# Row normalisation on one core: both loads ahead of the entry barrier and both stores on SyncE, in place of a first store on ScalarE

## The chip, the cores and the metric

The kernel runs on one core of one Trainium2 chip. The metric is device time in microseconds (us). A profiled execution has a span, from its first recorded instruction to its last; the measured time is a little longer than the span.

The core has compute engines that run their own instruction streams (here ScalarE, called ACT, and VectorE, called DVE, do the work), a SyncE (SP) that only issues transfers and waits, and 16 DMA engines that move data between the main memory (HBM) and the on-chip memory (SBUF). An engine that issues a transfer puts it into a queue of its own: q1 is SyncE's, q10 is ScalarE's.

## The reference

```python
def setup_inputs():
    batch, dim = 1024, 4096
    return {"x": np.random.randn(batch, dim).astype(np.float32), "axis": -1, "eps": np.float32(1e-12)}

def reference(x, axis, eps):
    norm = np.sqrt(np.sum(x ** 2, axis=axis, keepdims=True) + eps)
    return (x / norm).astype(np.float32)
```

Every one of the 1024 rows is divided by its Euclidean length. 16.78 MB are read and as much is written.

## The kernel before

The 1024 rows are 128 partitions times 8 rows. They are handled in two groups of R = 4 rows per partition; each group is one tile of 128 x 16384 floats (64 KB per partition), one load and one store.

```python
groups = []
for i in range(n_tiles):                       # n_tiles = 2
    g = RowGroups(nc, io, stats, scratch, D, R, eps_t)
    load = nc.sync.dma_start(out=g.flat(), in_=x_t[i])
    if i == 0:
        first_load_to_front(nc, load.ins)
    groups.append(g)

for i, g in enumerate(groups):
    g.square_dve(R - 1)      # sum of squares of row 3, on VectorE
    g.square_act(0)          # ... of row 0, on ScalarE
    g.norm(0)                # square root on ScalarE, reciprocal on VectorE
    g.scale(0)               # row times reciprocal, on VectorE, in place
    g.square_act(1)
    g.norm(1)
    g.norm(R - 1)
    g.scale(1)
    g.scale(R - 1)
    g.square_act(2)
    g.norm(2)
    if i < n_tiles - 1:
        g.scale_by_both(2)   # 7/8 of the row on ScalarE, 1/8 on VectorE
    else:
        g.scale(2)
    queue = nc.scalar if i < n_tiles - 1 else nc.sync
    store = queue.dma_start(out=out_t[i], in_=g.flat())
gpsimd_waits_for_last_store(nc, store.ins)
```

(The comments are added here.) A program starts with an entry barrier, at which every engine reports and waits for the others. The first load is moved ahead of SyncE's report to it:

```python
def first_load_to_front(nc, load):
    def move(program):
        blocks = program.main_func.blocks
        entry = blocks[0].instructions
        # ... cut: return if it is there already; find the load in its block (body, at)
        before = next(
            n for n, i in enumerate(entry)
            if i.engine == mybir.EngineType.SP and isinstance(i, mybir.InstDrain)
        )
        entry.insert(before, body.pop(at))
    nc.at_finalize(move)
```

At the end of the program SyncE waits for everything but the last store, and GpSimd alone waits for the last store (`gpsimd_waits_for_last_store`); this part is not changed.

Load 0, load 1, store 0 and store 1 are the names used below for the four transfers.

Of the kernel before, what the change touches and what calls it, by code (L numbers as in the profile page):

```python
# [79 lines left out]
        )  # L80


def first_load_to_front(nc, load):

# [6 lines that stand above are left out]
        if any(i.name == load.name for i in entry):  # L93
            return
        body = next(
            b.instructions
            for b in blocks
            if any(i.name == load.name for i in b.instructions)
        )
        at = next(n for n, i in enumerate(body) if i.name == load.name)  # L100
        assert not body[at].sync_info.on_wait
        before = next(
            n
            for n, i in enumerate(entry)
# [5 lines that stand above are left out]
# [72 lines left out]
@with_exitstack  # L182
def kernel(
    ctx: ExitStack,
    tc: tile.TileContext,
    x: bass.AP,
    axis: bass.AP,
    eps: bass.AP,
    out: bass.AP,
):  # L190
    nc = tc.nc
    P = nc.NUM_PARTITIONS

    assert isinstance(axis, int) and axis in (-1, len(x.shape) - 1)
    eps = float(eps)

    x = x.flatten_outer_dims()
    out_flat = out.flatten_outer_dims()
    N, D = x.shape
    R = 4  # L200
    assert N % (P * R) == 0
    n_tiles = N // (P * R)
    x_t = x.rearrange("(p t r) d -> t p (r d)", t=n_tiles, r=R)
    out_t = out_flat.rearrange("(p t r) d -> t p (r d)", t=n_tiles, r=R)

    io = ctx.enter_context(tc.tile_pool(name="io", bufs=n_tiles))
    scratch_pool = ctx.enter_context(tc.tile_pool(name="scratch", bufs=1))
    stats = ctx.enter_context(tc.tile_pool(name="stats", bufs=n_tiles))

    eps_t = scratch_pool.tile([P, 1], F32)  # L210
    nc.vector.memset(eps_t, eps)  # L211
    sq_act = scratch_pool.tile([P, D], F32)
    sq_dve = scratch_pool.tile([P, D], F32)
    scratch = {"act": sq_act, "dve": sq_dve}

    groups = []
    for i in range(n_tiles):
        g = RowGroups(nc, io, stats, scratch, D, R, eps_t)
        load = nc.sync.dma_start(out=g.flat(), in_=x_t[i])
        if i == 0:  # L220
            first_load_to_front(nc, load.ins)
        groups.append(g)

    for i, g in enumerate(groups):
        g.square_dve(R - 1)
        g.square_act(0)
        g.norm(0)
        g.scale(0)
# [8 lines that stand above are left out]
            g.scale_by_both(2)  # L237
        else:
            g.scale(2)
        queue = nc.scalar if i < n_tiles - 1 else nc.sync  # L240
        store = queue.dma_start(out=out_t[i], in_=g.flat())
    gpsimd_waits_for_last_store(nc, store.ins)


# [33 lines left out]
```

## Time and profile before

| | |
|---|---|
| time, median of 3 runs | 82.57 us (82.54 to 82.77) |
| span of the profiled execution | 80.7 us |
| bytes read from HBM / written to it | 16.78 MB / 16.78 MB |
| share of the DMA engines' span, q1 / q10 | 72.8% / 25.0% |
| load 0 issued | 0.00 us |
| load 1 issued | 0.78 us |
| compute on group 0 begins | 21.81 us |
| store 0 issued, on ScalarE | 38.71 us |
| compute on group 1 begins | 41.12 us |
| store 1 issued, on SyncE | 56.53 us |

Times within an execution count from the start of the span. In the profile's lines, "L33" is a line of the kernel, "ACTq" and "SPq" are issues of transfers by ScalarE and SyncE, a bracket at the end of a timeline line gives the idle time before the instruction and what ended it. A line of waits gives who waited for whom, then the total in us, how often, and the longest. In the strips of 40 slices each digit is the busy share of a fortieth of the span, in tenths.

### The profile page before, as it was taken

The page shows a single profiled execution, that of the slowest core. Times are in us where ns is not written, and L with a number is a line of the kernel's source. Part 1 is how long each engine was busy: PE and PEld are TensorE (multiplying, and loading weights), DVE is VectorE, ACT ScalarE, POOL GpSimd, SP SyncE. Part 2 cuts the span into 40 slices and gives each one's busy share as a digit, 9 for nine tenths or more (in the row PEclk, how much of TensorE's full clock was granted, in tenths as well). Part 3 has the DMA queues.
Part 4 walks back from the last instruction along what each step waited for, and adds up shares of the span by engine and source line. Part 5 has one row for each costly group of instructions (what it writes and reads, how often), then busy time and mean ns, then how long its engine had stood idle before and what let it go on. Part 6 is the DMA issues. An engine that isn't in the chain of part 4 may idle for free.

```text
span 80.7 us, 93 instructions
## 1 busy us (share of the span) xinstructions
DVE 26.8 (33%) x21; ACT 29.8 (37%) x23; POOL 0.2 (0%) x4
## 2 busy tenths in 40 slices
DVE  0000000000199599940069899979000000000000
ACT  6000000000199999989169699970000000000000
POOL 0000000000000000000000000000000000000000
DMA  9099999299999299999199909999938999938990
GB/s 520 32 487 520 520 520 455 97 487 520 520 520 455 97 487 520 520 520 487 65 487 520 520 32 487 520 520 520 520 162 357 520 520 520 520 162 357 520 520 0
DMA packets 576, 33.55 MB, mean 416 GB/s; under 512 B 64, under 2 KB 64, under 8 KB 64
## 3 DMA queue, kind: packets, MB, share of 16 engines
q1 hardware_dynamic: 432, 25.17, 72.8%
q10 hardware_dynamic: 144, 8.39, 25.0%
HBM read 16.78 MB, written 16.78 MB: 416 GB/s over the span
## 4 chain that ended last, share of the span: by engine, by line
DMA 50%; ACT 10%; DVE 9%; issue 0%
DMA xt<-in_x_dram 50%; ACT sq_act L33 9%; DVE sq_dve L42 6%; DVE xt L64 3%; ACT rstd L53 1%; DVE rstd L59 0%
## 5 line engine op out<-in xcount | busy, mean ns | idle before, releaser
L33 ACT ACTIVATE sq_act<-xt 128x4096 f32<-128x4096 f32 x6 | 21.6, 3608 | 22.2 <-DMA xt<-in_x_dram 22.2
L42 DVE SCALAR_TENSOR_TENSOR sq_dve<-xt 128x4096 f32<-128x4096 f32 x2 | 8.8, 4424 | 26.1 <-DMA xt<-in_x_dram 26.1
L64 DVE TENSOR_SCALAR xt<-xt,rstd 128x4096 f32<-128x4096 f32 x7 | 16.5, 2354 | 0.2
L72 ACT ACTIVATE xt<-xt,rstd 128x3584 f32<-128x3584 f32 x1 | 3.3, 3282 | 0.2 <-DVE rstd L59 0.2
L53 ACT ACTIVATE rstd<-ssq,eps_t 128x1 f32<-128x1 f32 x8 | 2.1, 290 | 0.9 <-DVE sq_dve L42 0.8
L59 DVE RECIPROCAL rstd<-rstd 128x1 f32<-128x1 f32 x8 | 1.3, 160 | 2.4 <-ACT rstd L53 2.4
L33 ACT ACT_TABLE_LOAD x1 | 1.3, 1283 | 0.8 <-PEq L259 0.8
L53 ACT ACT_TABLE_LOAD x1 | 1.3, 1283 | 0.0
L33 ACT ACTIVATION_READ_ACCUMULATOR sq_act<-xt 128x1 f32 x6 | 1.1, 185 | 0.0
L78 DVE TENSOR_SCALAR xt<-xt,rstd 128x512 f32<-128x512 f32 x1 | 0.5, 486 | 0.0
L211 DVE MEMSET eps_t<- 128x1 f32 x1 | 0.1, 59 | 0.9 <-PEq L259 0.9
L42 DVE DVE_READ_ACCUMULATOR sq_dve<-xt 128x1 f32 x2 | 0.2, 82 | 0.0
L259 POOL MEMSET const-bfloat16-1.0<- 128x1 bf16 x1 | 0.1, 101 | 0.0
L259 POOL MEMSET const-uint8-127<- 128x1 uint8 x1 | 0.1, 101 | 0.0
L259 POOL MEMSET const-float32-0.0<- 128x1 f32 x1 | 0.1, 98 | 0.2 <-issue 0.2
L259 POOL MEMSET const-float32-1.0<- 128x1 f32 x1 | 0.1, 98 | 0.0
## 6 DMA issues: line engine op xcount, KB each, us to landing
xt<-in_x_dram SPq DMA_DIRECT2D x2, 31.0
out_dram<-xt ACTq DMA_DIRECT2D x1, 24.9
out_dram<-xt SPq DMA_DIRECT2D x1, 24.0
```

Of the source, the lines that this page charges most:

```text
L33: self.nc.scalar.activation(out=sq_a, in_=self.x[:, r], func=ACT_F.Square, accum_out=self.ssq[:, r : r + 1],)
L42: self.nc.vector.scalar_tensor_tensor(out=sq_v, in0=self.x[:, r], scalar=1.0, in1=self.x[:, r], op0=ALU.mult, op1=ALU.mult, accum_out=self ...
L53: self.nc.scalar.activation(out=self.rstd[:, r : r + n], in_=self.ssq[:, r : r + n], func=ACT_F.Sqrt, bias=self.eps_t,)
L59: self.nc.vector.reciprocal(out=self.rstd[:, r : r + n], in_=self.rstd[:, r : r + n])
L64: self.nc.vector.tensor_scalar_mul(out=self.x[:, r], in0=self.x[:, r], scalar1=self.rstd[:, r : r + 1])
L72: self.nc.scalar.activation(out=self.x[:, r, :cut], in_=self.x[:, r, :cut], func=ACT_F.Copy, scale=rstd,)
L78: self.nc.vector.tensor_scalar_mul(out=self.x[:, r, cut:], in0=self.x[:, r, cut:], scalar1=rstd)
L211: nc.vector.memset(eps_t, eps)
L259: nc = _bacc.Bacc("TRN2", target_bir_lowering=False, num_devices=1)
```

## The change

Both loads are now moved ahead of SyncE's report to the entry barrier, and both stores are issued by SyncE. Before, only the first load was ahead of the barrier, and the first store was issued by ScalarE, right behind the scale that it shares with VectorE. The purpose is to have the second load queued as early as the first, and to keep ScalarE's stream free of transfers.

```diff
-def first_load_to_front(nc, load):
+def to_front(nc, load):
 ...
         load = nc.sync.dma_start(out=g.flat(), in_=x_t[i])
-        if i == 0:
-            first_load_to_front(nc, load.ins)
+        to_front(nc, load.ins)
         groups.append(g)
 ...
-        queue = nc.scalar if i < n_tiles - 1 else nc.sync
-        store = queue.dma_start(out=out_t[i], in_=g.flat())
+        store = nc.sync.dma_start(out=out_t[i], in_=g.flat())
     gpsimd_waits_for_last_store(nc, store.ins)
```

In the compiled program SyncE issues load 0 and load 1, then takes part in the barrier, then issues store 0 (which waits for VectorE and ScalarE) and store 1. ScalarE's stream loses its one transfer, and the scheduler also places the instructions of its second group differently: before, the first square is followed by two square roots, the first of which waits for VectorE's square; after, it is followed by one square root, which waits for ScalarE alone, and the other of the two comes after the second square.

## The prediction

> **What bounds the kernel now.** I read the page first, its busy times and its 40 slices, because they tell at once whether an engine or the transfers carry the span.
>
> ```profile
> span 80.7 us, 93 instructions
> DVE 26.8 (33%) x21; ACT 29.8 (37%) x23; POOL 0.2 (0%) x4
> DVE  0000000000199599940069899979000000000000
> ACT  6000000000199999989169699970000000000000
> DMA packets 576, 33.55 MB, mean 416 GB/s; under 512 B 64, under 2 KB 64, under 8 KB 64
> HBM read 16.78 MB, written 16.78 MB: 416 GB/s over the span
> ```
>
> No compute engine is busy for half of the span. Both are idle from the start to slice 10 and from slice 28 to the end. 33.55 MB must move, and 416 GB/s over 80.7 us is all of it. So I ask whether the transfers ever pause. The page's DMA row has digits between 0 and 9 that look like pauses, but rows of 64 KB are booked whole at their start, so a slice of 2 us holds one round of them or none; I don't read that row. I took the packet records of the same trace instead (each has a queue, a start, a duration and a size) and sorted the 512 packets of 64 KB into 32 rounds of 16, one per engine. Summarised, with times from the span's start:
>
> ```
> round  what                        starts         mean took
> 1      load 0, first row           1.00 to 1.40   3.11 us
> 2-8    load 0                      4.02 ...       2.42 us
> 9      load 1, first row          20.94 to 21.44  2.42 us
> 16     load 1, last row           37.84 to 38.34  2.42 us
> 17     store 0, first row         40.27 to 40.77  3.25 us
> 24     store 0, last row          58.03 to 58.36  2.42 us
> 25     store 1, first row         60.45 to 60.77  2.42 us
> 32     store 1, last row          77.35 to 77.68  2.42 us, last end 80.09
> ```
>
> Each round begins where the one before ends. From 1.0 us to 80.1 us all 16 engines always hold a row. The account of the span: 1.00 us to the first row, 32 rounds at 2.416 us between starts = 77.3 us, 0.69 us extra in round 1, 0.83 us extra in round 17, together 79.8 us, within 0.3 us of the last row's end at 80.09 (the engines' stagger), then 0.6 us for the last semaphores and the end, to 80.7. The time measured outside the span is 82.57 - 80.7 = 1.9 us.
>
> Then the timeline and the waits, for how near the compute comes to the transfers.
>
> ```profile
> 35.40 3.28 ACT L72 ACTIVATE xt<-xt,rstd 128x3584 f32<-128x3584 f32 x1 [0.23 <-DVE rstd L59]
> 38.71 0.37 ACTq L241 DMA_DIRECT2D out_dram<-xt  x1
> 41.12 3.62 ACT L33 ACTIVATE sq_act<-xt 128x4096 f32<-128x4096 f32 x1 [2.44 <-DMA xt<-in_x_dram]
> ```
> ```profile
> 54.15 2.35 DVE L64 TENSOR_SCALAR xt<-xt,rstd 128x4096 f32<-128x4096 f32 x1
> 56.53 0.35 SPq L241 DMA_DIRECT2D out_dram<-xt  x1
> ```
> ```profile
> SPq L241 <- DMA xt<-in_x_dram: 40.0, 1, 40.0
> SPq L241 <- DVE xt L64: 15.4, 1, 15.4
> SPq L273 <- DMA out_dram<-xt: 6.3, 1, 6.3
> ```
>
> Store 0 is issued at 38.71, the moment the shared scale ends (35.40 + 3.28 = 38.68), and its rows can start at 40.27, when load 1 is done with the engines: 1.56 us ahead. Store 1 is issued at 56.53 and its rows start at 60.45: 3.9 us ahead. SyncE waits for load 1 from just after its own second issue until 41.1 and then for VectorE until 56.5: it is free at 38.7, as far as engine work goes.
>
> **What the skill says.** The Trainium skill, "DMA: Bandwidth & Descriptors", section "Issuing engines are not separate DMA queues": transfers from ScalarE and SyncE end on the same 16 engines, and a second issuing engine saves only sequencer time. The trace agrees: q1 and q10 never give more than 16 rows at once. Its section "Where 436 GB/s comes from" puts the ceiling at 435 GB/s; 65,536 B in 2.418 us times 16 is 434 GB/s, so the rows run at it, and no arrangement of issues can shorten 32 rounds. (The same page's 358 GB/s for HBM is not what binds here; the rows measure more.) Its section "Queues, rings and completion order" says that an engine takes turns between the queues that have work. The trace shows that in one place: the completion packets of store 0 on q10 run at 62.9 to 63.2, one row of store 1 (2.4 us) after store 0's last row, in 15 of 16 engines. And "Perfetto Trace Analysis", section "DMA Instruction — HWDGE (DVE, Sync)", says the issue shown in a profile is descriptor generation and not data; here issues take 0.33 to 0.38 us, against 20 us to move the data.
>
> **The change, part by part.** One: load 1 moves ahead of the barrier. It is issued at about 0.40 us instead of 0.78, after load 0's 0.377 us issue. It sits behind load 0 in the same queue and its first row starts at 20.94, when load 0's eighth row ends; the pitch from round 8 to round 9 is 2.42 us, as everywhere. It was queued 20 us early and is now queued 20.4 us early. Worth: 0. The cost: SyncE arrives at the barrier some 0.33 us later (the duration of that issue), so ScalarE's table load at 0.78 and VectorE's memset at 0.85 move to about 1.1 to 1.2. Both are needed at 21.8, when load 0 has landed. Cost: 0. Load 0's own issue remains first, so the first row should still start at 1.0.
>
> Two: store 0 moves from ScalarE to SyncE. Its wait is now on the semaphores of both compute engines, seen from a third. SyncE took up store 1 about 0.03 us after VectorE's end (54.15 + 2.35 = 56.50 to 56.53), ScalarE took up store 0 0.03 us after its own end. So store 0 is issued at 38.7 either way, plus or minus 0.05 us, against the 1.56 us in hand. ScalarE is spared 0.37 us of issue at 38.71, while it idles 2.44 us for load 1. Worth: 0.
>
> Three: all four transfers are in one queue, in the order load 0, load 1, store 0, store 1. The order of rows is already that. Store 0's completion no longer waits for a row of store 1, so it should land at about 61.2 instead of 63.6; only SyncE's closing wait sees it, and the end waits for store 1. Worth: 0.
>
> Four, which the diff does not show but the compiled order does: the scheduler arranges ScalarE's second group anew. Before, after the first square it waits for VectorE's square (0.8 us) and takes two square roots; after, it takes one root and goes on to the next square, at about 45.2 instead of 45.98, and the root for VectorE's row follows at 49.0. VectorE's second reciprocal then waits until about 49.3 instead of 48.38; three times reciprocal and scale at 0.16 + 2.35 us and 0.04 us of gaps end at 56.9. Store 1 is issued about 0.4 us later, at 56.95, with 3.5 us in hand instead of 3.9. Cost: 0.
>
> Sum: 0. The one place where something can move is round 17, whose 0.83 us is the only avoidable loss between 4 and 80 us.
>
> **The rivals.** *The 0.83 us belongs to the change of queue.* Round 17 is the first use of q10, and round 1, the first use of q1, has an extra 0.69 us of the same size. In one warm queue it would vanish, and the time would be 82.57 - 0.8 = 81.75. For it: rounds 9 and 25 follow in already used queues and show no extra. Against it: rounds 9 and 25 also join transfers of the same direction, queued long before, while round 17 turns from reading HBM to writing it with only 1.56 us of lead. Either of these stays with the change, and then nothing is gained. I cannot separate the three from this trace; I give the queue 15%.
>
> *The single queue stalls on completions.* If a queue must confirm its HBM writes before the next row may start, store 1 would be held up behind store 0, by something like the 0.8 us again: 83.4. Against it: behind load 0 (round 9) there is no pause, and on the one engine whose store 0 completion went ahead of store 1's row (at 60.45) the row still started at once. 6%.
>
> *The transfers open a gap.* If store 0 were issued so late that load 1's rows ran out first, every microsecond would count in full. It needs an issue later by more than a part of the 1.56 us; a first row took 1.00 us from issue to start at the span's beginning, which leaves about 0.56 us. A semaphore hop is some 0.03 us. 4%. An earlier load 1 issue could also disturb the first rows of load 0 while they are being queued (1.00 to 1.40 us); I expect under 0.1 us.
>
> **Range and chances.** The centre is the time before, less a little for the first rival: 82.5. Repeats before lie within 82.54 to 82.77, so 82.1 to 82.9 holds the outcome "nothing moves" with room for some tenths in round 17; the two 0.8 us outcomes lie outside. 2% is 1.65 us, more than round 1 and round 17 lose together (1.52 us), so faster by 2% has almost nothing to come from: 0.01. Slower by 2% needs a gap that no view shows: 0.02. Same: 0.97.
>
> **What would show it.** Right: two issues on SyncE back to back before 0.8 us; ScalarE's table load at about 1.1; load 0 landing at 21.8 and load 1 at 41.1; store 0 issued at 38.7 on SyncE, its first rows still taking 3.2 us; its landing 2.4 us earlier; store 1 issued at about 56.95; all rows on one queue; the last row ending near 80.1. Wrong: rows of round 17 at 2.4 us (first rival, span 79.9), a longer round 25 (second), a start of round 17 later than the end of round 16 (third), or a changed first row.

## The result, and the profile after

| | before | after |
|---|---|---|
| time, median of 6 runs | 82.66 us (82.54 to 82.77) | 81.88 us (81.73 to 81.98) |
| span of the profiled execution | 80.7 us | 79.9 us |

The ratio is 0.990, with a 95% interval of 0.989 to 0.992. The change is a gain of 0.8 us, under the 2% mark, and 0.2 us below the range that was predicted. From the page of the changed kernel, first the span, the busy times and the DMA queues, in the same order as the page of before:

```profile
span 79.9 us, 93 instructions
DVE 26.7 (33%) x21; ACT 29.7 (37%) x23; POOL 0.2 (0%) x4
DMA packets 576, 33.55 MB, mean 420 GB/s; under 512 B 64, under 2 KB 64, under 8 KB 64
q1 hardware_dynamic: 576, 33.55, 97.6%
HBM read 16.78 MB, written 16.78 MB: 420 GB/s over the span
```

The same packets and bytes, all on one queue now, at 420 instead of 416 GB/s. Engines are as idle as before. So the 0.8 us came out of the transfers, and the packet records say where. Rounds are numbered as in the prediction (16 rows of 64 KB each, times in us from the span's start):

```
                               before                     after
round  what                    starts        mean took    starts        mean took
1      load 0, first row       1.00 - 1.40   3.11         1.01 - 2.04   2.97
16     load 1, last row       37.84 - 38.34  2.42        37.90 - 38.34  2.43
17     store 0, first row     40.27 - 40.77  3.25 (q10)  40.32 - 40.77  2.42 (q1)
18     store 0                43.55 - 43.87  2.42        42.73 - 43.19  2.42
25     store 1, first row     60.45 - 60.77  2.42        59.64 - 60.09  2.42
32     last end               80.09                      79.41
```

From round 2 to the start of round 17 the mean starts of the two executions lie within 0.05 us of each other. Then store 0's first row takes 3.25 us in one and 2.42 us in the other, and that is the whole difference: counted between the mean starts of rounds 16 and 18, the hand-over costs 0.84 us beyond two plain rounds before and 0.01 after. (Of the 0.83 us the span keeps 0.77: the rows of after run 0.05 us later from round 2 on, the slowest of the 16 engines ends 0.25 us behind their mean instead of 0.15, and the closing after the last row takes 0.53 instead of 0.61.)

The timeline of the changed kernel around that moment:

```profile
35.41 3.28 ACT L72 ACTIVATE xt<-xt,rstd 128x3584 f32<-128x3584 f32 x1 [0.23 <-DVE rstd L59]
38.71 0.35 SPq L239 DMA_DIRECT2D out_dram<-xt  x1
41.15 3.62 ACT L33 ACTIVATE sq_act<-xt 128x4096 f32<-128x4096 f32 x1 [2.46 <-DMA xt<-in_x_dram]
```

Issued at 38.71 as before, to the hundredth; only "SPq" stands where "ACTq" stood. Load 1 reaches ScalarE at 41.15 instead of 41.12. So the gain does not come from an earlier issue or an earlier load. ScalarE's wait of 0.8 us for VectorE's square is gone, as the new order of its instructions leads one to expect, but store 1 is issued only 0.03 us sooner for it (56.50) and its rows start 3.1 us later, so this does not shorten the span. The waits of SyncE's queue show the other side effect that was foreseen:

```profile
SPq L239 <- ACT xt L72: 2.8, 1, 2.8
SPq L271 <- DMA out_dram<-xt: 3.2, 1, 3.2
```

SyncE now waits for ScalarE's scale, and its closing wait for store 0 is 3.2 us instead of 6.3: 0.8 us of the first row and 2.4 us because store 0's completion no longer waits for a row of store 1.

### The profile page after: what moved, and what is told of

The parts are those of the page before. It is cut to its first block, busy times and chain, and to the rows that moved or that the text cites. A ratio compares the mean times of both kernels' runs of the same rounds, so it can differ in the third digit from the quotient of the medians.

```text
span 79.9 us, 93 instructions
## 1 busy us (share of the span) xinstructions
DVE 26.7 (33%) x21; ACT 29.7 (37%) x23; POOL 0.2 (0%) x4
## 4 chain that ended last, share of the span: by engine, by line
DMA 51%; ACT 10%; DVE 9%; SPq 0%; issue 0%
DMA xt<-in_x_dram 51%; ACT sq_act L33 9%; DVE xt L64 9%; ACT rstd L53 1%; SPq L219 0%; DVE rstd L59 0%
```

## Experiments

A hand-over is the place where the rows of one transfer follow those of another. Two numbers describe it. The **extra** of a hand-over is the mean start of the second round after it, minus that of the last round before it, minus two plain rounds (2 x 2.415 us). The **lead** is the time from the issue of the new transfer to the mean moment at which the old one's last row would end undisturbed. (It is counted to the mean of the 16 engines: 1.76 us for store 0 before, where the prediction counted 1.56 us to the first of them.) Extra and lead are of the one profiled execution; ratios are of timed runs, with their 95% intervals. The extra is a mean over the 16 engines, while the span ends with the slowest of them, so a run can lose more time than its extra says.

**Which half of the change.** The theory after the result was the first rival of the prediction, a cost of passing from q1 to q10; its own rival was the earlier load.

```diff
 # e1_stores_sp, against before
-        queue = nc.scalar if i < n_tiles - 1 else nc.sync
-        store = queue.dma_start(out=out_t[i], in_=g.flat())
+        store = nc.sync.dma_start(out=out_t[i], in_=g.flat())
```


> Only the second half of the change: both stores on SyncE; load 1 stays behind the barrier. Queue theory (the 0.83 us of round 17 belong to handing the engines from q1 to q10): the first row of store 0 takes 2.42 us, span 79.9, time 81.9, ratio 0.990. Load theory (the gain is the earlier load 1): round 17 stays at 3.25 us, span 80.7, time 82.6, ratio 1.000.

Measured: 81.84 us, ratio 0.990 (0.989 to 0.992), span 79.9, extra 0.01 us.

```diff
 # e2_loads_front, against before
-        if i == 0:
-            first_load_to_front(nc, load.ins)
+        to_front(nc, load.ins)
```


> Only the first half of the change: both loads ahead of the barrier; store 0 stays on ScalarE. Queue theory: the first row of store 0 takes 3.25 us as before, span 80.7, time 82.6, ratio 1.000. Load theory: span 79.9, time 81.9, ratio 0.990.

Measured: 82.59 us, ratio 1.000 (0.999 to 1.001), span 80.8, extra 0.79 us. The stores' queue is the whole change; the earlier load is worth nothing.

**First use, or any hand-over?** Next question: is q10 slow because it is new, because it is another queue, or because a load is followed by a store?

```diff
 # e3_store1_act, against after
-        store = nc.sync.dma_start(out=out_t[i], in_=g.flat())
+        queue = nc.sync if i < n_tiles - 1 else nc.scalar
+        store = queue.dma_start(out=out_t[i], in_=g.flat())
```


> The changed kernel with store 1, not store 0, on ScalarE: a hand-over from q1 to q10 that is also the first use of q10, but from a store to a store and queued some 3.9 us ahead. If any first use of q10 or any hand-over costs: the first row of store 1 (round 25) takes 3.25 us, span 80.7. If the cost needs the turn from reading to writing together with the hand-over, or a short lead: round 25 takes 2.42 us, span 79.9.

Measured: 81.89 us, ratio 0.992 (0.990 to 0.994), extra at round 25 0.01 us with a lead of 3.3 us. The first use of q10 and the passage to it are both free in this execution. In timed runs the passage is not always free: seven of the ten took 81.79 to 81.95 us, the other three 82.25 to 82.42; no trace shows where those three lost it.

```diff
 # e4_warm_act, against before
+    warm = scratch_pool.tile([P, 1], F32)
+    nc.scalar.dma_start(out=warm, in_=x_t[0][:, :1])
```


> The kernel before, plus one load of 128 x 4 bytes on ScalarE's queue at the start, 38 us ahead of store 0; nothing reads it. First-use theory (q10 is slow because store 0 is its first transfer): the first row of store 0 takes 2.42 us, span 79.9 plus the tiny load (under 0.2 us), time 81.9 to 82.1. Hand-over or lead theory: round 17 stays at 3.25 us, span 80.7 to 80.9, time 82.6 to 82.8.

Measured: 82.72 us, ratio 1.001 (1.000 to 1.001), extra 0.60 us. First use is out. The same run showed two more things. The 4-byte rows of the tiny load took turns with the 64 KB rows of load 0; the page's issues (KB, then us from issue to landing) say what that meant for it:

```profile
warm<-in_x_dram ACTq DMA_DIRECT2D x1, 0.5 KB, 23.5
```

0.5 KB took 23.5 us to land, while load 0 was not slowed: its rounds stay 2.42 us apart. And round 17 fell into two kinds of engines. On eleven the row took 3.06 to 3.45 us. Each of these started 0.002 us after the end of the row before. On the other five, where it came 0.12 to 0.19 us after that end, it took 2.46 us: coming a little late cost less than coming in time. (The records do not name the engine; the starts and ends left over are paired in their order.)

**Lead, or direction?** That made the time of issue a suspect. The shared scale is a dial for it: its cut between ScalarE and VectorE moves store 0's issue, and besides it only the length of the two parts. The first pair moves it on q10.

```diff
 # e5_half_act, against before         # e6_full_act, against before
-        cut = 7 * self.D // 8         -        cut = 7 * self.D // 8
+        cut = self.D // 2             +        cut = self.D    (VectorE's part is dropped)
```


> The kernel before (store 0 on ScalarE, q10) with its shared scale cut in half (2048 + 2048 instead of 3584 + 512 elements), so that it ends 1.3 us sooner: store 0 issued at about 37.4 instead of 38.71, 2.9 us instead of 1.56 us ahead of round 17's start. Lead theory (q10 needs more than 1.56 us of lead to take over without a pause, q1 does not): the extra of round 17 falls from 0.83 us to under 0.1, span 79.9, time 81.9, ratio 0.990. Turn theory (from q1 to q10 and from reading to writing at once): the extra stays 0.7 to 0.8 us, time 82.6, ratio 1.000.

Measured: 82.72 us, ratio 1.000 (0.999 to 1.001), extra 0.88 us at a lead of 3.0 us. An earlier issue does not help; now load 1's last row is the one that is stretched (3.14 us), and the store's first row only a little (2.57).

> The kernel before with the shared scale left to ScalarE whole (4096 elements): store 0 issued 0.43 us later, at about 39.15, on q10. Lead theory: each us of later issue costs a us, the extra of round 17 (with any idle before it) rises from 0.83 to 1.25 us, span 81.1, time 83.1, ratio 1.005. Turn theory: the extra is a fixed 0.7 to 0.8 us as long as the rows are there by 40.3, time 82.6, ratio 1.000.

Measured: the issue at 39.24, lead 1.27 us, and an extra of 0.24 us in the profiled execution, against 1.25 expected. So the lead theory, in which every later microsecond costs one, falls as well. The timed runs scatter: six of twenty, the profiled one (82.22) among them, took 82.14 to 82.28 us, the others 82.49 to 82.93; the ratio is 0.998 (0.996 to 0.999). So the extra of 0.24 us is that of a lucky run, and the median, 82.61, is near the kernel before and at the 82.6 of the turn theory; even the slowest run stays under the 83.1 of the lead theory.

```diff
 # e7_full_sp, against after: cut = self.D, as in e6_full_act
```


> The changed kernel (store 0 on SyncE, q1) with the shared scale left to ScalarE whole: store 0 issued at about 39.15, 1.1 us ahead of round 17. If one queue needs only some 1.0 us of lead (issue to first row at the span's start): extra of round 17 under 0.15 us, time 81.9, ratio 0.990. If q1 too is at the edge of its lead with 1.56 us: the extra rises to 0.4 us, time 82.3, ratio 0.995.

Measured: 82.14 us, ratio 0.994 (0.992 to 0.996), lead 1.31 us, extra 0.22 us: the engines stand still for 0.18 us on average before round 17. This is plain lateness. Being 0.51 us later cost 0.22, so, as an estimate, store 0 has some 0.3 us to spare on q1 in the changed kernel.

```diff
 # e8_store1_act_late, against e3_store1_act; the added result is not used
         else:
+            nc.vector.tensor_scalar_mul(
+                out=sq_dve[:, :2688], in0=g.x[:, 1, :2688], scalar1=g.rstd[:, 2:3])
             g.scale(2)
```


> Both loads in front, store 0 on SyncE, store 1 on ScalarE, and one added scale of 2688 elements into scratch on VectorE (1.6 us, its result is not used), so that store 1 is issued about 1.6 us ahead of its first row instead of 3.2 us: a hand-over from q1 to q10 from store to store, with the short lead of store 0 in the kernel before. Lead theory: the first row of store 1 (round 25) gets the extra 0.7 to 0.8 us, span 80.8, time 82.7, ratio 1.000. Turn theory: no extra, span 80.0, time 81.9, ratio 0.991.

Measured: 82.73 us, ratio 1.000 (0.999 to 1.001), lead 1.70 us, extra at round 25 0.86 us. A store behind a store, on the second queue, has the same pause as store 0 before. Direction is not needed for it. The next four runs sought the boundary.

```diff
 # e9_early_act, against before: row 2 of group 0 has no square, root and reciprocal
 # of its own; it is scaled by row 1's factor, so store 0 is ready sooner
-        rstd = self.rstd[:, r : r + 1]
+        rstd = self.rstd[:, r - 1 : r]        (in scale_by_both)
```


> The kernel before with the square, root and reciprocal of row 2 of group 0 left out (row 2 is scaled by row 1's factor), so that store 0 is issued on q10 at about 35.3, 4.9 us ahead of round 17 and while load 1 still has a whole row to come on every engine. Last-row theory (the pause comes when another queue's transfer arrives while the old queue is in its last row): no extra, or under 0.15 us, span 79.9, time 81.9, ratio 0.990. Turn theory (reading on q1 to writing on q10 costs, however early): extra 0.7 to 0.9 us, time 82.7, ratio 1.000.

Measured: 83.26 us, ratio 1.007 (1.005 to 1.008), lead 4.7 us, extra 1.09 us at round 17 and 0.43 at round 25. The last-row theory falls for a store behind a load.

```diff
 # e10_lead34_act, against e5_half_act: the square of row 2 of group 0 leaves out 704 elements
 # (cut: square_act takes the width as an argument)
-        g.square_act(2)
+        g.square_act(2, 3392 if i == 0 else 4096)
```


> The kernel before with the shared scale cut in half and the square of row 2 of group 0 taken over 3392 of 4096 elements, so that store 0 is issued on q10 at about 36.9, 0.9 to 1.5 us ahead of round 16's start, as store 1 was ahead of round 24's in the run with store 1 on ScalarE (0.7 to 1.2 us, no extra). Last-row theory: extra under 0.3 us, span 80.0 to 80.3, ratio 0.990 to 0.995. Turn theory: extra 0.8 us, span 80.8, ratio 1.000.

Measured: 83.22 us, ratio 1.006 (1.004 to 1.008), lead 3.7 us, extra 0.95 us at round 17 and 0.25 at round 25. The same verdict. The 0.25 and 0.43 us at round 25 in these two runs are a different loss: load 1 landed at 44.7 and 45.0 us instead of 41.1, because its completion on q1 came only after store 0's first row on q10 (on all 16 engines in e9_early_act, on 14 in e10_lead34_act), and so store 1 was issued at 60.1 and 60.4, too late.

```diff
 # e11_store1_act_mid, against e8_store1_act_late      # e12_store1_sp_late, against after
-   2688 elements                                      +   the added scale of 2688 elements
+   1024 elements                                      +   of e8_store1_act_late
```


> Store 1 on ScalarE again, with an added scale of 1024 elements on VectorE (0.75 us, result not used): store 1 issued about 2.3 us ahead of round 25, that is about 0.1 us after round 24, the last row of store 0, has begun. Last-row theory: extra 0.5 to 0.9 us in rounds 24 and 25, span 80.6 to 80.9, ratio 0.997 to 1.000. A theory that asks only for a lead above some 1.6 us: no extra, ratio 0.991.

Measured: 82.68 us, ratio 1.000 (0.999 to 1.001), lead 2.67 us, extra at round 25 0.85 us.

> The changed kernel (everything on SyncE) with the added scale of 2688 elements on VectorE, so that store 1 is issued about 1.5 us ahead of round 25 as in the late run on ScalarE, but on the queue that is already running. If only another queue's arrival costs: no extra in round 25, span 79.9, ratio 0.990. If any transfer that arrives in the last row costs when it follows a store: extra 0.8 us, ratio 1.000.

Measured: 81.87 us, ratio 0.990 (0.988 to 0.992), lead 1.79 us, extra at round 25 0.01 us. This is the cleanest pair of the study. The timelines of store 1 in e8_store1_act_late and in e12_store1_sp_late:

```profile
58.19 0.37 ACTq L243 DMA_DIRECT2D out_dram<-xt  x1
```
```profile
58.08 0.34 SPq L242 DMA_DIRECT2D out_dram<-xt  x1
```

and the landings on their pages (us from issue to landing, the last figure; the SPq line of the second is the median of both stores):

```profile
out_dram<-xt ACTq DMA_DIRECT2D x1, 22.6
```
```profile
out_dram<-xt SPq DMA_DIRECT2D x2, 21.8
```

Behind the same rows, within 0.11 us of the same time, with the same bytes: 22.6 us from issue to landing on the second queue, 21.8 on the running one.

**Is the running queue free at every lead?** If so, the second queue would explain everything.

```diff
 # e13_half_sp, against after          # e14_early_sp, against e9_early_act
-        cut = 7 * self.D // 8         -  both stores as in before (ScalarE, SyncE)
+        cut = self.D // 2             +  both stores on SyncE
```


> The changed kernel with the shared scale cut in half: store 0 issued on q1 at about 37.5, as in the run with the half cut on ScalarE, which had an extra of 0.88 us. If the second queue is the cause: no extra at round 17, span 79.9, ratio 0.990. If it is the store that arrives in load 1's last row: extra 0.8 to 0.9 us, ratio 1.000.

Measured: 82.64 us, ratio 1.000 (0.999 to 1.001), lead 2.9 us, extra 0.57 us. The running queue is not free here. The whole gain is gone, though the extra is less than 0.84: the last row ends 0.46 us later on the slowest engine than on average, against 0.25 in the changed kernel. Load 1 arrives 0.71 us later than in the changed kernel:

```profile
37.63 0.35 SPq L239 DMA_DIRECT2D out_dram<-xt  x1
41.86 3.62 ACT L33 ACTIVATE sq_act<-xt 128x4096 f32<-128x4096 f32 x1 [4.26 <-DMA xt<-in_x_dram]
```

> The run with the square, root and reciprocal of row 2 of group 0 left out, but with both stores on SyncE: store 0 issued on q1 at about 35.8. On q10 load 1 landed only at 45.0 and the extra was 1.1 us, with 0.4 us more at store 1. If the second queue is the cause: load 1 lands at 41.1, no extra at rounds 17 and 25, span 79.9, ratio 0.990. If an early store disturbs the load on any queue: span 80.8 to 81.6, ratio 1.000 to 1.006.

Measured: 82.99 us, ratio 1.005 (1.003 to 1.006), lead 4.9 us, extra 1.06 us, none at round 25. The timeline of e14_early_sp:

```profile
35.69 0.35 SPq L240 DMA_DIRECT2D out_dram<-xt  x1
42.21 3.62 ACT L33 ACTIVATE sq_act<-xt 128x4096 f32<-128x4096 f32 x1 [6.55 <-DMA xt<-in_x_dram]
```

Store 0 is queued 3.0 us earlier than in the changed kernel, in the same queue, behind load 1, and load 1 arrives 1.06 us later (42.21 against 41.15). Its last row takes 3.47 us instead of 2.42. Order in a queue does not keep a later store from slowing the load ahead of it.

```diff
 # e15_load1_act, against before; the squares on the still empty tile are added work
+            nc.vector.memset(g.x[:, 0], 1.0)
+            (five ScalarE squares on g.x[:, 0])
-        load = nc.sync.dma_start(out=g.flat(), in_=x_t[i])
+            load = nc.scalar.dma_start(out=g.flat(), in_=x_t[i])     (for i == 1; both stores too)
```


> Load 1 issued on ScalarE's queue at about 19.4 us, after added squares on its still empty tile (not part of the computation), 1.5 us ahead of load 0's end; both stores on ScalarE too. Only round 9 is read: the compute behind it comes in another order and store 0 late, so the span is over 83. If any hand-over at a short lead costs: the first row of load 1 takes 3.1 to 3.3 us. If it costs only where the new queue stores: 2.42 us.

A miss: the memset took 3.47 us and load 1 was issued at 21.76, after load 0's end. Its first row, on idle engines, took 3.01 us, as load 0's does; nothing is learnt of a hand-over between loads. Store 0 too met idle engines here: issued at 59.37, it started at 60.21 and its first row took 2.46 us. So the 0.83 us is not what a store needs to start on idle engines.

**The width of the free window.** The last three runs used the dial again.

> The changed kernel with the shared scale cut at 3/4 (3072 + 1024): store 0 issued on q1 at about 38.3, 2.0 us ahead of round 17. If the disturbance grows from a lead of 1.6 us in proportion to the earliness (0.57 us at 2.65): extra 0.2 us, span 80.2, ratio 0.993. If the window is wider: extra under 0.05, ratio 0.990.

Measured, cut at 3/4: 81.99 us, ratio 0.992 (0.989 to 0.994), lead 2.24 us, extra 0.08 us.

> The changed kernel with the shared scale cut at 5/8 (2560 + 1536): store 0 issued on q1 at about 37.9, 2.35 us ahead. In proportion: extra 0.4 us, span 80.4, ratio 0.996. If the cost is all or nothing once the store arrives inside load 1's last row early enough: 0.55 us or under 0.05.

Measured, cut at 5/8: 82.29 us, ratio 0.996 (0.995 to 0.997), lead 2.61 us, extra 0.50 us. The profiled execution was one of the slower ones (82.59 of 82.14 to 82.67), so the extra of a typical run is smaller.

> The kernel before with the shared scale cut at 15/16 (3840 + 256): store 0 issued on q10 at about 38.95, 1.3 us ahead. If the second queue has a free window too, only later: extra under 0.15 us, span 80.1, ratio 0.992. If it goes straight from disturbed to late: extra between 0.24 and 0.6 us, span 80.3 to 80.6, ratio 0.996 to 0.999.

Measured, on q10 with the cut at 15/16: 82.71 us, ratio 1.000 (0.999 to 1.002), lead 1.52 us, extra 0.46 us. Ten engines had a row of 2.46 us after a stop of 0.19 to 0.24 us; on the other six the row started 0.002 us after the one before and took 3.11 to 3.44. The second queue goes straight from disturbed to late; behind a load no free window was found on it.

All hand-overs of a load to a store, and of a store to a store, with their leads and extras in us (e15_load1_act apart; each from one profiled execution):

```
load 1 -> store 0     q1 -> q1: 1.31 0.22 | 1.67 to 1.81 0.01 to 0.03 (six kernels, after among them)
                                2.24 0.08 | 2.61 0.50 | 2.91 0.57 | 4.89 1.06
                      q1 -> q10: 1.27 0.24 | 1.52 0.46 | 1.73 to 1.78 0.60 to 0.84 (before, e2, e4)
                                3.03 0.88 | 3.68 0.95 | 4.70 1.09
store 0 -> store 1    q1 -> q1: 1.79 0.01 | 3.1 to 3.5 0.00 to 0.03
                      q1 -> q10: 1.70 0.86 | 2.67 0.85 | 3.32 0.01
                      q10 -> q1: 0.52 0.43 | 0.73 0.25 (e9, e10: store 1 late) | 3.3 to 4.1 0.00 to 0.05
```

## Why the prediction was wrong

**What bounds the kernel** was read rightly. The rows stay at 2.42 us, no engine matters, and the account of the span (first row, 32 rounds, round 1, round 17, closing) holds after too, with one term changed.

**Part one** (load 1 ahead of the barrier, worth 0) was right: e2_loads_front measured 1.000. Its side effect was larger than said: load 1's issue took 0.43 us, and ScalarE's table load came at 1.26 instead of 1.1 to 1.2, for nothing that matters. The first rows of load 0 spread more (1.01 to 2.04 instead of 1.00 to 1.40), but end as they did (4.10 to 4.54 against 4.02 to 4.52).

**Part two** (store 0 to SyncE) is where it failed. The issue time was right, 38.71. "Worth: 0" was not. The step that failed is the weighing of round 17's 0.83 us, in which "Either of these stays with the change" was said of the turn from reading to writing and of the short lead, and the queue was given 15%. Neither of the two makes the pause by itself: at the same lead of 1.7 to 1.8 us the turn costs 0.01 to 0.03 us in one queue and 0.60 to 0.84 us across two, and a store behind a store pays 0.86 us across two. The argument against the queue rested on round 25 of the kernel before, a passage from q10 to q1 without extra. It was a passage with a lead of 4.1 us, more than a whole row; e3_store1_act and e8_store1_act_late show that store to store the lead decides whether a passage can be free (3.3 us) or not (1.7 us). The likeness of round 1 and round 17, which spoke for the queue, does not hold: a first use can be free (e3), a queue used before still has the pause (e4), and a store that starts on idle engines has no long first row (e15). So "first use of q10" in the first rival fell, and the change of queue at a short lead stands.

**The first rival** was right in its number, 81.75 us against 81.88 measured, and right that one queue removes the pause at this lead. It was not right as a rule: "In one warm queue it would vanish" holds only for a store queued at the right moment. On the same queue, with the store issued 1.1 us earlier, the extra is 0.57 us; 3 us earlier it is 1.06.

**Part three** (store 0's completion no longer waits) was right: it landed at 60.5 us, 61.2 predicted less the 0.8 of round 17. **Part four** was right that it costs 0, wrong in size: store 1 was issued at 56.50, not 56.95. VectorE's first reciprocal of the group no longer waited 0.36 us for a root and began at 45.49 instead of 45.91, and the roots came at 48.69 rather than 49.0. **The second rival** (completions stall one queue) fell: round 25 has an extra of 0.01 us. **The third** (a gap) did not occur, and the slack of 0.56 us was oversized: e7_full_sp puts it at some 0.3 us.

**What stays open.** Why an early store stretches the row of the load ahead of it, and why a store on a second queue has a long first row of its own when it comes within the last 1.8 us (store behind store at 2.67 us too), is not shown. The records give each row's start and end, not what the engine does within a row. In every run the queue and the engine that issues changed together, so whether the second queue or ScalarE as the issuer makes the pause is not separated. From store to store, leads between 2.7 and 3.3 us on two queues and above 1.8 but below 3.1 us on one, and hand-overs from load to load on two queues, were not measured.

## What to carry to other kernels

When transfers bound a kernel and the engines never seem to pause, list the rows in order of time and compare their durations where one transfer follows another: a first row of 3.25 us among rows of 2.42 was all that this change had to gain. Try such a hand-over within one queue, and vary the moment of the issue by a microsecond on both sides, since earlier was worse here, by up to 1.1 us. Keep the moment that measures best, and measure again when the computation changes: this gain rests on a window of lead from about 1.7 to 2.2 us, which a faster computation would leave.

## What was not expected of the hardware

A store queued 4.9 us ahead in the same queue delayed the load in front of it by 1.06 us. A transfer on a second queue that came 0.12 to 0.19 us after the last row had ended cost less (2.46 us for its first row) than on the engines where it came in time (3.06 to 3.45 us, e4_warm_act). A load of 0.5 KB took 23.5 us to land when it shared the engines with rows of 64 KB.
